# Tail of an encoder layer: where the last rows are scaled, added and summed

## The chip, the cores and the metric

The kernel runs on one core of one Trainium2 chip. A core has a matrix engine (TensorE, "PE" in the profile), three engines for elementwise work (VectorE or "DVE", ScalarE or "ACT", GpSimd or "POOL"), a queue engine that only issues transfers (SyncE, "SP"), an on-chip memory of 128 partitions (SBUF) and accumulation banks behind TensorE (PSUM). The metric is device time in microseconds of the whole program.

## The reference

The reference is one layer of an encoder on 512 positions of width 1024, in float32:

```python
h = _rmsnorm(x, g_pre_mix)
...                                  # retention and gating branches, merged
x = x + _rmsnorm(merged @ w_out, g_post_mix)
h2 = _rmsnorm(x, g_pre_ffn)
x = x + _rmsnorm(_conv_gated_mlp(h2, w_up, conv_w, conv_b, w_down), g_post_ffn)
```

with `_rmsnorm(y, g) = y / sqrt(mean(y*y) + EPS) * g` along each row. Only the last line concerns us. Call the result of `w_down` y, and x after the first half x1. Each row of the output is `x1 + y * g_post_ffn * (mean(y*y) + EPS) ** -0.5`.

## The kernel before

The 512 positions are four token tiles of 128 rows, t = 0 to 3; a row's 1024 columns are two halves of 512. Weights stream from DRAM through SyncE's queue; ScalarE and VectorE split every float32 matrix into a high and a low part, and TensorE multiplies three products of those parts for each tile. Some of the products use a Strassen-like scheme with seven products, whose results are then combined by VectorE.

The output matrix of the MLP is made in two column halves. The first half (columns 0 to 511) is finished early: `first_share` (L1418) multiplies it by `g_post_ffn` into a tile `zg[t]` and puts its mean of squares into column 0 of the small tile `qn[t]`. The second half (columns 512 to 1023) is finished at the very end, tile by tile, by `token(t)` (L1434), in the order 0, 2, 1, 3. Each call

- loads the two halves of x1 of this tile from DRAM (`xt`, L1440, on SyncE's queue);
- lets TensorE add the last 24 products to two banks, 12 for each quarter of 256 columns (`add_whole`, L1370);
- `sums(i)` for quarter i: VectorE adds bank and earlier part into z (L1452), and ScalarE squares z and sums along the row into column 2 + i of `qn[t]` (L1454). An ACTIVATE with a sum shows in the trace as two instructions, the second an accumulator read;
- `weighted(i)`: VectorE multiplies z by `g_post_ffn` into `zs_` (L1459);
- `first_sum`: VectorE adds column 2 and EPS to column 0 (L1462, one element per row);
- `scale`: VectorE adds column 3 (`s_2`, L1469), and POOL raises it to the power -0.5 (`sc`, named `qr` in the trace, L1470);
- `rows(t', ...)` for the tile t' before it: VectorE computes `zg * sc + x1` and `zs_ * sc + x1` in place, one instruction per half (L1502; the last tile's second half in two quarters), and stores each piece on SyncE's or ScalarE's queue (L1505).

After the last tile `rows` is called for it too. So the rows of tile 0 are made during tile 2, those of tile 2 during tile 1, those of tile 1 during tile 3.

A scheduler orders the instructions of each engine when the program is built, by trace order and by when it thinks that operands are ready. `tc.keep_in_program_order` (called `pin` here) queues an instruction behind the one that was traced before it on its engine; it is applied in tiles 1 and 3 to VectorE's instructions. `tc.issue_after(ins)` queues all instructions of a block, on `ins`'s engine, behind `ins`, without waiting for it to finish. Every engine runs its instructions in the order given; waits between engines are semaphores. Tiles of SBUF named by `blk` come from a pool of 66 buffers that are taken again when their last reader is done.

Of the kernel before, what the change touches and what calls it, by code (L numbers as in the profile page):

```python
# [12 lines left out]
AF = mybir.ActivationFunctionType  # L13
ALU = mybir.AluOpType

P = 128
D = 1024
S = 512
NT = S // P
# [30 lines left out]
def tile_block(ctx: ExitStack, tc, xT, x, wall, par, cs, wsp, bsp, gpost, gffn, out):  # L50
    nc = tc.nc
# [6 lines left out]
    def nm(s):  # L58
        uid[0] += 1
        return f"{s}_{uid[0]}"  # L60

    def blk(dt=F32, n="blk", shape=(P, S)):
        return sb.tile(list(shape), dt, tag="blk", bufs=NBLK, name=nm(n))
# [17 lines left out]
    def tmp(n="tmp", shape=(P, S)):  # L81
        return sb.tile(list(shape), F32, tag="tmp", bufs=6, name=nm(n))

    def halves(n):
        return [blk(n=n), blk(n=n)]

    def small(n, w, bufs=2):
        return sb.tile([P, w], F32, tag=n, bufs=bufs, name=nm(n))
# [4 lines left out]
    def const(n, shape):  # L93
        return sb.tile(list(shape), F32, tag=n, bufs=1, name=n)
# [4 lines left out]
    def two(t):  # L99
        return t.rearrange("p (n c) -> p n c", n=2)  # L100
# [5 lines left out]
    def in_turn(o):  # L106
        return o.rearrange("p (c n) -> p n c", n=2)
# [16 lines left out]
    i = 0  # L124
    while i < NW:
        pair = [(f, i) for f in FORMS]
        if i == SV0:
# [3 lines left out]
            i = U0  # L131
# [6 lines left out]
        elif i == UP0 + 2 * COUPLES[0][0]:  # L138
# [3 lines left out]
            i = UP0 + 2 * COUPLES[-1][1] + 2  # L142
# [10 lines left out]
    v = nc.vector  # L153
# [123 lines left out]
    def w_get(look=LOOK):  # L277

        i = w_pos[0]
        w_pos[0] += 1  # L280
        room = 2 * look + (2 if w_size(units[i]) == 2 else 0)
        n = sum(w_size(u) for u in units[i : w_pos[1]])
        while w_pos[1] < len(units) and (w_pos[1] <= i or n + w_size(units[w_pos[1]]) <= max(room, 9 if look == LOOK else 0)):
            u = units[w_pos[1]]
            w_ready[w_pos[1]] = w_unit(u)
            w_pos[1] += 1
            n += w_size(u)
        return w_ready.pop(i)
# [106 lines left out]
    for k in range(KD):  # L395
# [4 lines left out]
        xt = xts[k]  # L400
# [55 lines left out]
    for t in range(NT):  # L456
        for n in range(2):
            xt = blk(n="x0")
            nc.sync.dma_start(xt, x[t, :, n * S : (n + 1) * S])
            nc.scalar.activation(  # L460
                out=xt, in_=xt, func=AF.Square, accum_out=ss[:, 4 * n + t : 4 * n + t + 1]
# [18 lines left out]
    for c in range(19, 1, -2):  # L480
        v.scalar_tensor_tensor(
            out=lc, in0=lc, scalar=1.0 / c, in1=lb, op0=ALU.add, op1=ALU.mult
        )
    v.scalar_tensor_tensor(out=lc, in0=lc, scalar=1.0, in1=la, op0=ALU.add, op1=ALU.mult)
    with behind():
        v.tensor_scalar(out=lg, in0=lgt, scalar1=0.0, scalar2=None, op0=ALU.min)
    v.scalar_tensor_tensor(
        out=lg, in0=lc, scalar=-2.0, in1=lg, op0=ALU.mult, op1=ALU.add
# [12 lines left out]
    for i, op in enumerate((ALU.max, ALU.min)):  # L501
        v.tensor_scalar(
            out=near[:, i * P : (i + 1) * P], in0=dist[:, P : 2 * P], scalar1=0.0, scalar2=None, op0=op
# [5 lines left out]
    zt = const("zt", [P, H, NT])  # L509
# [465 lines left out]
    for j in range(UW):  # L975
# [3 lines left out]
        i = v.tensor_mul(two(u), in_turn(o), two(rbc)).ins  # L979
# [135 lines left out]
    x1 = [[dp_.tile([P, S], F32, tag=f"x1_{t}{n}", name=f"x1_{t}{n}") for n in range(2)] for t in range(NT)]  # L1115
# [36 lines left out]
    def turn(t, zs):  # L1152
        c = slice(t * 64, (t + 1) * 64)
        pf = []
        for n in range(2):
            p = ps()
            for f in range(4):
                pf.append(p[:, f * P : (f + 1) * P])
                nc.tensor.transpose(pf[-1], zs[n][:, f * P : (f + 1) * P], ident)
        for k in range(KD):  # L1160
            high = nc.scalar.activation(
                out=two(h2h[k])[:, :, c], in_=in_turn(pf[k]), func=AF.Copy, scale=col(FFNG + k)
            )
        for k in range(KD):
            last = v.scalar_tensor_tensor(
                out=two(h2l[k])[:, :, c], in0=in_turn(pf[k]), scalar=col(FFNG + k), in1=as32(two(h2h[k])[:, :, c]),
                op0=ALU.mult, op1=ALU.subtract,
            )
        return pf, high.ins, last.ins
# [26 lines left out]
    for t in range(NT):  # L1196
        acc = [dn_.finish(t, 0)]
        if t > 1:
            rows, _, last = turn(t - 2, zs[t - 2])
            if t == 2:  # L1200
                h2_rows(0, rows)
            with tc.issue_after(last):
                zs[t - 1] = scaled(*zs[t - 1])
        acc.append(dn_.finish(t, 1))
        zs[t], squared, ended = norms(t, acc)
        if t == 0:
            zs[0] = scaled(*zs[0])
    with tc.issue_after(squared):
        h2_rows(1, rows)
# [103 lines left out]
    i = 0  # L1313
# [46 lines left out]
    def add_whole(m, t, gs, ws, last=False):  # L1360

        c = slice(t * P, (t + 1) * P)
        for n, b in enumerate(((M2, M3), (M4, M8))[t // 2]):
            o = m[b][:, (t % 2) * 256 : (t % 2 + 1) * 256]
            for g, (wh, wl) in zip(gs, ws):
                for k in range(2):
                    f = slice(k * S + n * 256, k * S + (n + 1) * 256)
                    ah, al = whole[2 * g + k]
                    for i, (a_, w_) in enumerate(((ah, wh), (ah, wl), (al, wh))):
                        nc.tensor.matmul(  # L1370
                            o, a_[:, c], turns(w_[:, f]), start=b == M8 and t == 2 and g == k == i == 0,
                            stop=last and g == gs[-1] and k == 1 and i == 2, skip_group_check=True,
                        )
# [41 lines left out]
    qn = [small("q", 4, 4) for _ in range(NT)]  # L1415
# [13 lines left out]

    m, ww = {}, []  # L1430
    e1, uu, xx, yy = (blk(n="e") for _ in range(4))
    ahead = []

    def token(t):  # L1434

        if not ww:
            ww.extend([w_get(), w_get()])
        xt = halves("x1")
        for n in range(2):
            nc.sync.dma_start(xt[n], x1[t][n])  # L1440
        add_whole(m, t, (0, 1), ww, True)
        z, zs_ = blk(n="z"), blk(n="zs")
        last, ahead[:] = list(ahead), []
        banks = (((M2, e1), (M3, xx)), ((M4, uu), (M8, yy)))[t // 2]
        halves_ = slice(0, 256), slice(256, 512)
        end = t in (1, NT - 1)
        pin = tc.keep_in_program_order if end else (lambda i: i)

        def sums(i):
            b, e = banks[i]  # L1450
            f = halves_[t % 2]
            pin(v.tensor_add(z[:, halves_[i]], m[b][:, f], e[:, f]))  # L1452
            j = tmp("junk")
            nc.scalar.activation(  # L1454
                out=j[:, :256], in_=z[:, halves_[i]], func=AF.Square, scale=D ** -0.5, accum_out=qn[t][:, 2 + i : 3 + i]
            )

        def weighted(i):
            pin(v.tensor_mul(zs_[:, halves_[i]], z[:, halves_[i]], gpf[1][:, halves_[i]]))  # L1459

        def first_sum():
            pin(v.scalar_tensor_tensor(  # L1462
                out=qn[t][:, 0:1], in0=qn[t][:, 2:3], scalar=EPS, in1=qn[t][:, 0:1], op0=ALU.add, op1=ALU.add
            ))

        sc, s_2 = small("qr", 1, 4), small("qs", 1, 4)

        def scale():
            pin(v.tensor_add(s_2, qn[t][:, 0:1], qn[t][:, 3:4]))  # L1469
            nc.gpsimd.tensor_tensor(out=sc, in0=s_2, in1=nhalf[:, 0:1], op=ALU.pow)  # L1470

        sums(0)
        if t == NT - 1:
            weighted(0)
            sums(1)
            first_sum()
            rows(*last, (0,), pin)
            scale()
            rows(*last, (1,), pin)
            weighted(1)  # L1480
        else:
            weighted(0)
            first_sum()
            if end:
                rows(*last, (0,), pin)
            sums(1)
            if last:
                rows(*last, (1,) if end else (0,), pin)
            scale()
            weighted(1)  # L1490
            if last and not end:
                rows(*last, (1,))
        ahead[:] = t, xt, zs_, sc

    def rows(t, xt, zs_, sc, which, pin=lambda i: i):

        zt = (zg[t], zs_)
        for i, (a, b) in enumerate(((0, 512), (512, 768), (768, 1024)) if t == NT - 1 else ((0, 512), (512, 1024))):
            if a // S in which:
                f = slice(a % S, a % S + b - a)  # L1500
                o = zt[a // S][:, f]
                pin(v.scalar_tensor_tensor(  # L1502
                    out=o, in0=o, scalar=sc, in1=xt[a // S][:, f], op0=ALU.mult, op1=ALU.add
                ))
                (nc.sync, nc.scalar)[i % 2].dma_start(out[t, :, a:b], o)  # L1505

    def after6():
        v.tensor_add(uu, m[M6], e1)
        v.tensor_sub(xx, m[M5], uu)
        token(0)  # L1510
# [15 lines left out]
    for t in (2, 1, 3):  # L1526
        token(t)
# [133 lines left out]
```

## Time and profile before

| | us |
|---|---|
| median of 3 runs | 785.31 (785.30 to 785.34) |
| the profiled execution | 785.08 |
| its span | 783.3 |
| TensorE busy | 775.6 |
| VectorE busy | 626.5 |
| ScalarE busy | 467.8 |
| POOL busy | 104.0 |

The span is the time from the first to the last recorded instruction; the execution is 1.78 us longer than it. Times in the views are microseconds from the span's start. A timeline row gives start, duration, engine, line of the code, operation, and written from read tiles with their shapes; brackets hold the idle time ahead of it and what ended it. A row with "x2" merges two instructions. "SPq" and "ACTq" are queues on which transfers are issued, so such a row shows the issue and not the transfer itself.

### The profile page before, as it was taken

Reading aid. Unit: us, or ns where it says so; the run is one execution under the profiler, and the core shown is the slowest. Engines: PE = TensorE matmul, PEld = TensorE weight load, DVE = VectorE, ACT = ScalarE, POOL = GpSimd, SP = SyncE. Lnnn points to the kernel's source line nnn. Section 1 sums busy time; section 2 is a strip of 40 time slices with the busy share of each in tenths; the row PEclk is TensorE's granted clock in tenths of the full one; section 3 lists DMA queues with packets and bytes.
Section 4 is the critical chain, followed back from the end, with each engine's and each line's share of the span. In section 5 each row is a group of like instructions: output and inputs, shape, how many; then the busy total and the mean of one; then the engine's idle time right before and its main releaser. Section 6 shows DMA issues by size and latency. Waiting matters only on the chain.

```text
span 783.3 us, 13258 instructions
## 1 busy us (share of the span) xinstructions
PE 775.6 (99%) x5067; PEld 720.3 (92%) x5067; DVE 626.5 (80%) x1067; ACT 467.8 (60%) x848; POOL 104.0 (13%) x132
## 2 busy tenths in 40 slices
PE   9999999999999999999999999999999999999996
PEld 8888998998899999999998998999999998999996
DVE  7467887788786877867765679989999889877987
ACT  7555558689385544444444776657777578644542
POOL 0040001130012111032211200001111012200001
PEclk9999999999999999999999999999999999999999
DMA  8782224453123333223459111425555365632244
GB/s 293 260 266 88 81 82 162 108 133 126 55 106 108 108 108 108 106 84 108 138 161 344 57 69 39 122 108 141 141 149 149 108 196 114 170 114 108 108 162 162
DMA packets 35889, 104.78 MB, mean 134 GB/s; under 512 B 4401, under 2 KB 6321, under 8 KB 35825
## 3 DMA queue, kind: packets, MB, share of 16 engines
q1 hardware_dynamic: 27936, 87.81, 31.8%
q0 software_dynamic: 7024, 14.95, 9.0%
q10 hardware_dynamic: 864, 1.18, 0.4%
q8 instruction: 39, 0.64, 0.3%
q14 instruction: 26, 0.20, 0.1%
HBM read 91.34 MB, written 4.19 MB: 122 GB/s over the span
## 4 chain that ended last, share of the span: by engine, by line
PE 98%; DVE 1%; ACT 0%; POOLq 0%; issue 0%; POOL 0%; DVEq 0%
PE ps L917 22%; PE ps L291 13%; PE ps L293 13%; PE ps L292 13%; PE ps L1354 11%; PE ps L746 5%; PE ps L625 4%; PE ps L627 4%; PE ps L626 4%; PE ps L1089 2%; PE ps L1091 2%; PE ps L1090 2%; PE ps L1370 2%; PE ps L1011 1%; PE ps L411 1%; PE ps L393 0%
## 5 line engine op out<-in xcount | busy, mean ns | idle before, releaser
L116 DVE TENSOR_TENSOR wl<-raw,wh 128x1024 fp32r<-128x1024 f32 (+1 forms) x88 | 100.6, 1152 | 56.1 <-issue 20.6
L97 ACT ACTIVATE wf<-raw 128x512 fp32r<-128x512 f32 x126 | 75.6, 624 | 83.8 <-PE ps L292 37.1
L97 ACT ACTIVATE wh<-raw 128x1024 fp32r<-128x1024 f32 (+2 forms) x92 | 89.1, 981 | 28.9 <-DMA raw<-wall 15.5
L917 PE MATMUL ps<-sh,wf 128*128 128x256 f32 x576 | 105.3, 275 | 0.0
L116 DVE TENSOR_TENSOR wf<-raw,wf 128x512 fp32r<-128x512 f32 x126 | 93.3, 754 | 14.9 <-ACT wf L97 14.7
L917 PEld LDWEIGHTS ps<-sh,wf 128*128 128x128 f32 x576 | 91.7, 192 | 0.8 <-ACT u L97 0.2
L291 PE MATMUL ps<-h2h,wh 128*128 128x512 f32 (+1 forms) x256 | 90.7, 354 | 0.0
L293 PE MATMUL ps<-h2h,wl 128*128 128x512 f32 (+1 forms) x256 | 90.4, 353 | 0.0
L292 PE MATMUL ps<-h2l,wh 128*128 128x512 f32 (+1 forms) x256 | 90.4, 353 | 0.0
L917 PE MATMUL ps<-sl,wf 128*128 128x256 f32 x288 | 79.3, 275 | 0.0
L1354 PE MATMUL ps<-dh,fh 128*128 128x256 f32 x216 | 59.5, 276 | 0.0
L1354 PE MATMUL ps<-dh,fl 128*128 128x256 f32 x216 | 59.5, 275 | 0.0
L1354 PE MATMUL ps<-dl,fh 128*128 128x256 f32 x216 | 59.4, 275 | 0.0
L917 PEld LDWEIGHTS ps<-sl,wf 128*128 128x128 f32 x288 | 55.3, 192 | 0.4
L97 ACT ACTIVATE dh<-raw 128x768 fp32r<-128x768 f32 (+1 forms) x36 | 33.6, 950 | 33.5 <-DVE raw L224 17.6
L293 PEld LDWEIGHTS ps<-h2h,wl 128*128 128x128 f32 x256 | 48.6, 190 | 5.1
L291 PEld LDWEIGHTS ps<-h2h,wh 128*128 128x128 f32 x256 | 48.7, 190 | 4.5
L292 PEld LDWEIGHTS ps<-h2l,wh 128*128 128x128 f32 x256 | 48.7, 190 | 4.4
L627 PE MATMUL ps<-wh,xl 128*128 128x512 f32 x128 | 48.6, 379 | 0.0
L626 PE MATMUL ps<-wl,xh 128*128 128x512 f32 x128 | 48.5, 379 | 0.0
L625 PE MATMUL ps<-wh,xh 128*128 128x512 f32 x128 | 48.5, 380 | 0.0
L917 PE MATMUL ps<-xh,wf 128*128 128x256 f32 x240 | 43.8, 276 | 0.0
(343 smaller groups left out, 2185.8 us busy)
## 6 DMA issues: line engine op xcount, KB each, us to landing
raw<-wall SPq DMA_DIRECT2D x144, 512.0 KB, 3.6
x<-x SPq DMA_DIRECT2D x24, 256.0 KB, 5.9
fl<-gp POOLq DMA_DIRECT2D x12, 256.0 KB, 4.0
swap<-qkraw POOLq DMA_DIRECT2D x16, 128.0 KB, 4.3
x<-x POOLq DMA_DIRECT2D x8, 256.0 KB, 2.3
fl<-fs POOLq DMA_DIRECT2D x8, 256.0 KB, 3.3
xT<-xT SPq DMA_DIRECT2D x7, 256.0 KB, 5.5
xT<-xT POOLq DMA_DIRECT2D x4, 256.0 KB, 4.0
```

The lines of the kernel that those rows point to most:

```text
L97: return nc.scalar.activation(out=o, in_=i, func=AF.Copy)
L116: low[0] = nc.vector.tensor_sub(lo, src, as32(hi)).ins
L291: nc.tensor.matmul(o, ah, bh, start=start, stop=False, skip_group_check=skip)
L292: nc.tensor.matmul(o, ah, bl, start=False, stop=False, skip_group_check=skip)
L293: nc.tensor.matmul(o, al, bh, start=False, stop=stop, skip_group_check=skip)
L625: nc.tensor.matmul(acc[t], xh[k][:, c], turns(wh[:, f]), start=k == 0, stop=False)
L626: nc.tensor.matmul(acc[t], xh[k][:, c], turns(wl[:, f]), start=False, stop=False)
L627: part_end[0] = nc.tensor.matmul(acc[t], xl[k][:, c], turns(wh[:, f]), start=False, stop=k == KD - 1)
L746: nc.tensor.matmul(bank[t], a_[:, c], turns(w_[:, f]), start=first and k == i == 0, stop=last and k == 3 and i == 2, skip_group_check=True,)
L917: self.last = nc.tensor.matmul(o, w_[:, c], a_, start=first and k == n == 0, stop=k == 3 and n == 2, skip_group_check=True,)
L1089: nc.tensor.matmul(o, ah, turns(bh), start=k == 0, stop=False)
L1354: nc.tensor.matmul(o, a_[:, c], turns(w_[:, f]), start=j == t == i == 0, stop=j == DP - 1 and i == 2 and n not in (M2, M3, M4), skip_group ...
```

## The change

Three things are changed, all in the tail:

1. Tile 0's rows are no longer made by VectorE. ScalarE scales each half in place (`Copy` with `sc` as scale), and a transfer issued by POOL adds x1 into it, straight from DRAM (`accum_op=ALU.add`). x1 of tile 0 is therefore not loaded into SBUF. The two finished halves are stored by SyncE, in tile 3, queued behind the loads of x1 for tile 3.
2. In tile 3, the rows of tile 1 are placed otherwise among the pinned instructions: the first half ahead of `sums(0)`, the second half ahead of `sums(1)`. Before, both came behind `sums(1)`.
3. In tile 3, the squares of the last quarter are summed on VectorE: `tensor_tensor_reduce` multiplies z by itself, scales by 1/1024, adds up along the row starting from column 0 of `qn[t]`, and writes `s_2`. ScalarE's square and VectorE's addition of column 3 go; `first_sum` now comes between `z` and this instruction.

```diff
     e1, uu, xx, yy = (blk(n="e") for _ in range(4))
-    ahead = []
+    ahead, kept = [], []
 
     def token(t):
 
         if not ww:
             ww.extend([w_get(), w_get()])
-        xt = halves("x1")
-        for n in range(2):
-            nc.sync.dma_start(xt[n], x1[t][n])
+        xt = halves("x1") if t else x1[t]
+        for n in range(2 if t else 0):
+            loaded = nc.sync.dma_start(xt[n], x1[t][n]).ins
+        if t == NT - 1:
+            with tc.issue_after(loaded):
+                for n in range(2):
+                    nc.sync.dma_start(out[0, :, n * S : (n + 1) * S], kept[0][n])
         add_whole(m, t, (0, 1), ww, True)
...
+        sc, s_2 = small("qr", 1, 4), small("qs", 1, 4)
+
         def sums(i):
             b, e = banks[i]
             f = halves_[t % 2]
             pin(v.tensor_add(z[:, halves_[i]], m[b][:, f], e[:, f]))
             j = tmp("junk")
+            if t == NT - 1 and i:
+                first_sum()
+                pin(v.tensor_tensor_reduce(
+                    out=j[:, :256], in0=z[:, halves_[i]], in1=z[:, halves_[i]], scale=1.0 / D, scalar=qn[t][:, 0:1],
+                    op0=ALU.mult, op1=ALU.add, accum_out=s_2,
+                ))
+                return
...
-        sc, s_2 = small("qr", 1, 4), small("qs", 1, 4)
-
         def scale():
-            pin(v.tensor_add(s_2, qn[t][:, 0:1], qn[t][:, 3:4]))
+            if t < NT - 1:
+                pin(v.tensor_add(s_2, qn[t][:, 0:1], qn[t][:, 3:4]))
             nc.gpsimd.tensor_tensor(out=sc, in0=s_2, in1=nhalf[:, 0:1], op=ALU.pow)
 
-        sums(0)
         if t == NT - 1:
+            rows(*last, (0,), pin)
+            sums(0)
             weighted(0)
+            rows(*last, (1,), pin)
             sums(1)
-            first_sum()
-            rows(*last, (0,), pin)
             scale()
-            rows(*last, (1,), pin)
             weighted(1)
         else:
+            sums(0)
             weighted(0)
             first_sum()
             if end:
...
     def rows(t, xt, zs_, sc, which, pin=lambda i: i):
 
         zt = (zg[t], zs_)
+        if t == 0:
+            for n in which:
+                nc.scalar.activation(out=zt[n], in_=zt[n], func=AF.Copy, scale=sc)
+                nc.gpsimd.dma_start(zt[n], xt[n], accum_op=ALU.add)
+            kept.append(zt)
+            return
```

## The prediction

> **What bounds the kernel now.** I read three views: the page, for what carries the span as a whole; the chain of waits of the last 20 us, because the change touches only the tail; then the timelines of VectorE, TensorE, POOL, ScalarE and SP there.
>
> ```profile
> PE 775.6 (99%) x5067; PEld 720.3 (92%) x5067; DVE 626.5 (80%) x1067; ACT 467.8 (60%) x848; POOL 104.0 (13%) x132
> PE 98%; DVE 1%; ACT 0%; POOLq 0%; issue 0%; POOL 0%; DVEq 0%
> ```
>
> TensorE carries the program, and the change removes nothing from it. In the tail it is otherwise. "z(t,n)" is L1452 for token tile t and half n, "w(t,n)" the weighting L1459, "rows(t,n)" L1502, "q" L1462, "s_2" L1469. The tiles go 0, 2, 1, 3. TensorE:
>
> ```profile
> 769.42 0.28 PE L1370 MATMUL ps<-wh,fl 128*128 128x256 f32 x1
> 770.76 0.28 PE L1370 MATMUL ps<-wh,fl 128*128 128x256 f32 x1
> 772.10 0.28 PE L1370 MATMUL ps<-wh,fl 128*128 128x256 f32 x1
> 776.12 0.28 PE L1370 MATMUL ps<-wh,fl 128*128 128x256 f32 x1
> ```
>
> These are the last matmuls for z(2,0), z(2,1), z(1,0) and z(3,1); the last one ends at 776.40. VectorE, from tile 0's rows on:
>
> ```profile
> 768.58 0.69 DVE L1514 TENSOR_TENSOR e<-ps,e 128x512 f32<-128x512 f32 x1
> 769.35 0.75 DVE L1502 SCALAR_TENSOR_TENSOR zg<-zg,qr,x 128x512 f32<-128x512 f32 x1
> ...
> 770.35 0.75 DVE L1502 SCALAR_TENSOR_TENSOR zs<-zs,qr,x 128x512 f32<-128x512 f32 x1
> ...
> 772.41 0.16 DVE L1469 TENSOR_TENSOR qs<-q 128x1 f32<-128x1 f32 x1
> 772.49 0.42 DVE L1452 TENSOR_TENSOR z<-ps,e 128x256 f32<-128x256 f32 x1
> 772.94 0.42 DVE L1459 TENSOR_TENSOR zs<-z,gpf 128x256 f32<-128x256 f32 x1
> 773.48 0.16 DVE L1462 SCALAR_TENSOR_TENSOR q<-q 128x1 f32<-128x1 f32 x1
> 773.57 0.75 DVE L1502 SCALAR_TENSOR_TENSOR zg<-zg,qr,x 128x512 f32<-128x512 f32 x1
> 774.24 0.42 DVE L1452 TENSOR_TENSOR z<-ps,e 128x256 f32<-128x256 f32 x1
> 774.58 0.74 DVE L1502 SCALAR_TENSOR_TENSOR zs<-zs,qr,x 128x512 f32<-128x512 f32 x1
> 775.24 0.16 DVE L1469 TENSOR_TENSOR qs<-q 128x1 f32<-128x1 f32 x1
> 775.31 0.42 DVE L1459 TENSOR_TENSOR zs<-z,gpf 128x256 f32<-128x256 f32 x1
> 775.64 0.42 DVE L1452 TENSOR_TENSOR z<-ps,e 128x256 f32<-128x256 f32 x1
> 776.10 0.43 DVE L1459 TENSOR_TENSOR zs<-z,gpf 128x256 f32<-128x256 f32 x1
> 776.44 0.42 DVE L1452 TENSOR_TENSOR z<-ps,e 128x256 f32<-128x256 f32 x1
> 776.78 0.15 DVE L1462 SCALAR_TENSOR_TENSOR q<-q 128x1 f32<-128x1 f32 x1
> 776.84 0.74 DVE L1502 SCALAR_TENSOR_TENSOR zg<-zg,qr,x 128x512 f32<-128x512 f32 x1
> 777.51 0.16 DVE L1469 TENSOR_TENSOR qs<-q 128x1 f32<-128x1 f32 x1
> 777.58 0.74 DVE L1502 SCALAR_TENSOR_TENSOR zs<-zs,qr,x 128x512 f32<-128x512 f32 x1
> 778.25 0.42 DVE L1459 TENSOR_TENSOR zs<-z,gpf 128x256 f32<-128x256 f32 x1
> 778.77 0.75 DVE L1502 SCALAR_TENSOR_TENSOR zg<-zg,qr,x 128x512 f32<-128x512 f32 x1
> ```
>
> The reader is to see that VectorE hardly pauses from 773.48 to 778.67 (778.25 + 0.42). z(3,1) starts at 776.44, 0.04 behind the last matmul, and at the same moment VectorE comes free (0.34 behind w(3,0)): both limits meet there. Behind it, rows(1,0) at 776.84 and rows(1,1) at 777.58 fill the time in which ScalarE squares z(3,1) and POOL takes the root: they cost nothing where they stand. The rest of the tail:
>
> ```profile
> 775.54 0.60 POOL L1470 TENSOR_TENSOR qr<-qs,nhalf 128x1 f32<-128x1 f32 x1 [2.27 <-DVE qs L1469]
> 777.81 0.93 POOL L1470 TENSOR_TENSOR qr<-qs,nhalf 128x1 f32<-128x1 f32 x1 [1.67 <-DVE qs L1469]
> 776.95 0.42 ACT L1454 ACTIVATE junk<-z 128x256 f32<-128x256 f32 x1 [0.28 <-DVE q L1462]
> 777.27 0.20 ACT L1454 ACTIVATION_READ_ACCUMULATOR junk<-z 128x1 f32 x1
> 780.34 0.33 SPq L1505 DMA_DIRECT2D out<-zs  x1
> ```
>
> The chain is z(3,1), square, s_2, root, rows(3) from 778.77, store at 780.34; from z(3,1) to rows(3,0) it takes 2.33 us.
>
> **The change, part by part.**
>
> *Tile 0's rows leave VectorE.* Two instructions go (0.75 each, 769.35 and 770.35), 1.5 us of VectorE work. How much reaches the end? z(2,1) can then start right behind its matmuls (770.76 + 0.28 = 771.04, before at 771.42). z(1,0) cannot start before 772.10 + 0.28 = 772.38; with the 0.04 lag that is 772.42, against 772.49 before. So 0.07 of the 1.5 us is left; the remainder turns into waiting for TensorE. Bounds: 0 (a longer lag) to 0.07; I take 0.05, close to the lag seen at z(3,1).
>
> *The same rows on ScalarE and POOL.* The nearest rows:
>
> ```profile
> L97 ACT ACTIVATE wf<-raw 128x512 fp32r<-128x512 f32 x126 | 75.6, 624 | 83.8 <-PE ps L292 37.1
> L264 POOL DMA_DIRECT2D sb<-wall x4 | 3.6, 1072 | 12.0 <-DVE sl L116 10.7 <-ACT sh L97 1.3
> sb<-wall POOLq DMA_DIRECT2D x4, 256.0 KB, 6.0
> 772.72 0.55 POOL L1470 TENSOR_TENSOR qr<-qs,nhalf 128x1 f32<-128x1 f32 x1 [3.40 <-DVE qs L1469]
> 770.47 0.42 ACT L1454 ACTIVATE junk<-z 128x256 f32<-128x256 f32 x1 [2.45 <-DVE z L1452]
> 770.69 1.85 SPq L1440 DMA_DIRECT2D x<-x  x4
> ```
>
> Two copies of 0.62 from 769.35 (tile 0's scale is there, as its row on VectorE shows) end near 770.6. ScalarE had idled 2.45 us before 770.47, so the square of tile 2 slips by about 0.1; its sum is wanted at 772.4. L264 is the same kind of transfer, 256 KB from DRAM added into SBUF: 1.07 us of POOL each, 6.0 to landing. POOL would issue from about 770.0 to 772.1, and the next root is wanted at 772.4: cost 0, covered by POOL's idle time. Without this cover (rival C) it is dear. The sums land by about 777; both stores wait on SP for them, and behind those the stores of tiles 2, 1 and 3. The last of these is issued near 780 or later, so cost 0. Two loads of 256 KB fall away; tile 1's and 3's loads are issued from 770.69 at the latest known, or earlier since there is less ahead of them: cost 0.
>
> *The new order in tile 3.* All its VectorE instructions are pinned in program order. Now rows(1,0) stands ahead of z(3,0), and rows(1,1) ahead of z(3,1). But rows(1,0) needs tile 1's root, which ended at 775.54 + 0.60 = 776.14. With 0.05 gained: root 776.09, rows(1,0) 776.12. VectorE idles from about 775.6, where z(3,0) stood before. Then by the spacings above: z(3,0) + 0.67 = 776.79 (776.84 to 777.51); w(3,0) + 0.46 = 777.25; rows(1,1) + 0.34 = 777.59; z(3,1) + 0.67 = 778.26. That is 1.82 later than before, and TensorE has been done for 1.9 us. The two rows instructions are no longer hidden: they stand in front of the chain that they used to fill.
>
> *One instruction sums the squares.* Gone are square, accumulator read and s_2 (776.95 to 777.67); q now comes behind z(3,1): 778.60, and the sum waits for its result: 778.60 + 0.16 + 0.03 = 778.79. The trace has no such sum. Bounds: 0.42 (a 128x256 product, L1459) and 0.75 (twice as many elements, L1502); I take 0.52, since ScalarE's square and accumulator read take 0.52 together (776.95 to 777.47) against 0.42 for the square alone. It ends at 779.31. The root starts 0.14 behind s_2 in the rows (777.67 to 777.81): 779.45. Its price lies between 0.55 and 0.93; the 0.93 had rows(1,1), 0.74 long, running beside its start, the 0.55 and 0.60 only w or z. Beside it now is only w(3,1), so 0.58: 780.03, rows(3,0) at 780.06. From z(3,1) the chain takes 1.80 instead of 2.33: 0.53 won.
>
> [...]
>
> **Sum.** 1.82 - 0.53 = +1.29 (780.06 - 778.77), and behind rows(3,0) nothing changes. A second count of VectorE: 0.45 idle at rows(1,0), 0.4 idle under the last root (0.1 before), some 0.2 of dependent gaps and 0.45 of new sum against s_2, less 0.05 at the start: about +1.3 too. Span 783.3 + 1.3 = 784.6; the profiled execution took 785.08, so 786.37. The median, 785.31, lies 0.23 above that execution: 786.6, or +0.16%. A measurement of this kernel can tell about 0.2%, 1.57 us, from no change: my forecast is a small loss inside it.
>
> **The rivals.**
>
> *B, the sum or the last root dearer.* The sum costs 0.75, or the root 0.93: +1.5 to +1.9, 786.8 to 787.2. For it: neither has an exact row. Against: VectorE's L1502 reads two SBUF operands 512 wide in 0.75, only 0.06 more than L1514, as wide with one operand in PSUM (0.69); and long work of VectorE no longer stands beside the root. The sum costs 0.23 more at 0.75 (chance 0.10), the root 0.35 more at 0.93 (0.08). [...]
>
> *C, slower by more: the root of tile 2 gets stuck.* If ScalarE's copies come behind tile 2's squares (771.08 + 0.45 + 0.52 = 772.05), the first transfer is issued from 772.67, ahead of that root on POOL, and rows(2,0) waits: 772.67 + 1.07 + 0.56 = 774.3 instead of 773.5. It decides once the root starts after 772.9; price about +0.75 on top, 787.3. Against: the copies are ready at 769.35, tile 2's first z not before 769.42 + 0.28 + 0.04 + 0.42 = 770.16.
>
> *D, the new order costs nothing.* Were tile 1's root early enough for both rows to fit ahead of 776.40, only the shorter chain stays: -0.5, 784.8. Against: they need 2 x 0.67 and the root ended at 776.14.
>
> *E, the 1.5 us reach the end.* 785.31 - 1.5 = 783.8. Against: 772.38.
>
> **Chances.** Forecast 0.55 (0.07 of it above 786.88), B 0.18 (0.12 above), C 0.15 (0.14 above), D 0.07, E 0.05 (0.02 of it faster by over 0.2%). So faster 0.02, within 0.65, slower 0.33. The forecast's own range is 786.3 to 786.9 (sum 0.42 to 0.65, root 0.55 to 0.65); with B and most of C 785.7 to 787.4, which leaves out D, E and the top of C.
>
> **What would show it.** Right: VectorE idle before rows(1,0) near 776.1; z(3,1) near 778.3, with nothing of TensorE within 1.5 us; z(3,1) to rows(3,0) about 1.8. Wrong: z(3,1) near 776.5 (D), rows(2,0) after 774 (C), a sum of 0.7 or a last root of 0.9 (B). What would upset it all is another order on VectorE than the pins give.

## The result, and the profile after

The changed kernel takes 786.39 us (median of 22 runs, 785.76 to 787.24), the kernel before 785.33 (median of 22 runs beside them, 784.47 to 786.13). The ratio is 1.0015, with a 95% interval of 1.0008 to 1.0021: slower by 0.6 to 1.6 us, and within 0.2% by its median. The forecast was 786.6.

The ratios in this document leave out two single executions that took 1365.76 us (old order put back, below) and 2903.89 us (sum alone).

The profiled execution took 786.03, with a span of 784.2. Executions of one kernel differ by more than the change does to the tail (the 22 runs of before lie 1.66 us apart, the tail changes by 1.25), and in the nine profiles of this document the last matmul ends anywhere between 775.95 and 779.30; here it came 0.45 us earlier than in the profile of before. So I compare the tail from the end of the last matmul on, and call X the time from there to the start of rows(3,0). Line numbers move with each edit: in after, z is L1458, w L1472, q L1475, the sum L1462, rows L1520, the root L1482, tile 0's copies L1512 and its adding transfers L1513. First the busy times and the chain of the page of after, then rows of the timeline of its TensorE and VectorE (start, duration, instruction):

```profile
PE 774.9 (99%) x5067; PEld 719.2 (92%) x5067; DVE 626.0 (80%) x1066; ACT 468.3 (60%) x848; POOL 105.5 (13%) x134
...
PE 98%; DVE 1%; DMA 0%; ACT 0%; issue 0%; POOLq 0%; POOL 0%; ACTq 0%; DVEq 0%
```

```profile
775.67 0.28 PE L1370 MATMUL ps<-wh,fl 128*128 128x256 f32 x1
771.96 0.42 DVE L1458 TENSOR_TENSOR z<-ps,e 128x256 f32<-128x256 f32 x1
...
774.79 0.42 DVE L1472 TENSOR_TENSOR zs<-z,gpf 128x256 f32<-128x256 f32 x1
775.65 0.75 DVE L1520 SCALAR_TENSOR_TENSOR zg<-zg,qr,x 128x512 f32<-128x512 f32 x1 [0.44 <-POOL qr L1482]
776.32 0.42 DVE L1458 TENSOR_TENSOR z<-ps,e 128x256 f32<-128x256 f32 x1
776.77 0.42 DVE L1472 TENSOR_TENSOR zs<-z,gpf 128x256 f32<-128x256 f32 x1
777.12 0.74 DVE L1520 SCALAR_TENSOR_TENSOR zs<-zs,qr,x 128x512 f32<-128x512 f32 x1
777.78 0.41 DVE L1458 TENSOR_TENSOR z<-ps,e 128x256 f32<-128x256 f32 x1
778.11 0.15 DVE L1475 SCALAR_TENSOR_TENSOR q<-q 128x1 f32<-128x1 f32 x1
778.30 0.48 DVE L1462 CUSTOM_DVE_ANT_0 junk<-z,q 128x256 f32<-128x256 f32 x1
778.71 0.08 DVE L1462 DVE_READ_ACCUMULATOR2_ANT qs<- 128x1 f32 x1
778.71 0.42 DVE L1472 TENSOR_TENSOR zs<-z,gpf 128x256 f32<-128x256 f32 x1
779.57 0.75 DVE L1520 SCALAR_TENSOR_TENSOR zg<-zg,qr,x 128x512 f32<-128x512 f32 x1 [0.44 <-POOL qr L1482]
```

The last matmul ends at 775.67 + 0.28 = 775.95. VectorE then is in the middle of rows(1,0), which it began 0.44 us late because it waited for tile 1's root. z(3,1) starts at 777.78, which is 1.83 behind the last matmul (0.04 before). From there to rows(3,0) it takes 1.79 (2.33 before). X is 779.57 - 775.95 = 3.62, against 2.37: a loss of 1.25 in the tail. Behind rows(3,0) hardly anything changes: to the end of the span 4.63, before 4.53, with spans given to 0.1.

The other engines in the timeline of after, and two rows of its transfers (KB of each, us from issue to landing):

```profile
768.90 0.72 ACT L1512 ACTIVATE zg<-zg,qr 128x512 f32<-128x512 f32 x1 [1.33 <-POOL qr L1482]
769.53 0.71 ACT L1512 ACTIVATE zs<-zs,qr 128x512 f32<-128x512 f32 x1
769.98 0.91 POOL L1513 DMA_DIRECT2D zg<-x  x1 [1.12 <-ACT zg L1512]
770.60 1.21 POOL L1513 DMA_DIRECT2D zs<-x  x1
772.05 0.56 POOL L1482 TENSOR_TENSOR qr<-qs,nhalf 128x1 f32<-128x1 f32 x1 [0.24 <-DVE qs L1481]
775.02 0.60 POOL L1482 TENSOR_TENSOR qr<-qs,nhalf 128x1 f32<-128x1 f32 x1 [2.41 <-DVE qs L1481]
778.93 0.60 POOL L1482 TENSOR_TENSOR qr<-qs,nhalf 128x1 f32<-128x1 f32 x1 [3.32 <-DVE qs L1462]
775.88 0.33 SPq L1444 DMA_DIRECT2D out<-zs  x1
```

```profile
zg<-x POOLq DMA_DIRECT2D x1, 256.0 KB, 3.9
zs<-x POOLq DMA_DIRECT2D x1, 256.0 KB, 5.3
```

Tile 0's copies and adding transfers run where they were expected, and POOL is free 0.24 us before the next root is wanted. Tile 0's second half is stored at 775.88, long before the last store.

### The profile page after: what moved, and what is told of

Same layout as the page of the kernel before. It is cut to its first block, busy times and chain, and to the rows that moved or that the text cites. A ratio compares the mean times of both kernels' runs of the same rounds, so it can differ in the third digit from the quotient of the medians.

```text
span 784.2 us, 13253 instructions
## 1 busy us (share of the span) xinstructions
PE 774.9 (99%) x5067; PEld 719.2 (92%) x5067; DVE 626.0 (80%) x1066; ACT 468.3 (60%) x848; POOL 105.5 (13%) x134
## 4 chain that ended last, share of the span: by engine, by line
PE 98%; DVE 1%; DMA 0%; ACT 0%; issue 0%; POOLq 0%; POOL 0%; ACTq 0%; DVEq 0%
PE ps L917 22%; PE ps L291 13%; PE ps L292 13%; PE ps L293 13%; PE ps L1354 11%; PE ps L746 5%; PE ps L625 4%; PE ps L627 4%; PE ps L626 4%; PE ps L1370 2%; PE ps L1090 2%; PE ps L1089 2%; PE ps L1091 2%; PE ps L1011 1%; PE ps L411 1%; PE ps L818 0%
```

## The experiments

All seven kernels compute the whole layer. This table takes X from each timeline; the ratio is to the kernel before, run beside it.

| kernel | z(3,1) behind the last matmul | z(3,1) to rows(3,0) | X | ratio, 95% interval |
|---|---|---|---|---|
| before | 0.04 | 2.33 | 2.37 | |
| after | 1.83 | 1.79 | 3.62 | 1.0015 (1.0008 to 1.0021) |
| old order put back in after | 0.03 | 2.60 | 2.63 | 1.0002 (0.9993 to 1.0011) |
| order alone | 1.90 | 2.32 | 4.22 | 1.0023 (1.0014 to 1.0032) |
| tile 0 alone | 0.03 | 2.34 | 2.37 | 1.0001 (0.9992 to 1.0010) |
| sum alone | 0.04 | 2.59 | 2.63 | 1.0005 (0.9996 to 1.0014) |
| z and w of tile 3 first, in after | 1.29 | 1.79 | 3.08 | 1.0015 (1.0006 to 1.0024) |
| w(3,1) first, in before | 0.04 | 2.14 | 2.18 | 1.0002 (0.9993 to 1.0011) |
| order alone, store elsewhere | 1.90 | 2.00 | 3.90 | 1.0017 (1.0005 to 1.0030) |

A ratio's interval here is some 0.7 us to either side, so the ratios tell the order's kernels from before and not one small step from another. X tells those apart, from one profiled execution each; the reading relies on X. Kernels with the same order and the same instructions behind the last matmul repeat it to the hundredth (2.37 twice, 2.63 twice).

### The old order put back in the changed kernel

```diff
         if t == NT - 1:
-            rows(*last, (0,), pin)
             sums(0)
             weighted(0)
-            rows(*last, (1,), pin)
             sums(1)
+            rows(*last, (0,), pin)
             scale()
+            rows(*last, (1,), pin)
             weighted(1)
```

> The changed kernel with tile 1's rows put back behind z(3,1); tile 0's rows on ScalarE and the sum on VectorE stay. Let X be the time from the end of the last matmul to the start of rows(3,0): 2.37 us before (776.40 to 778.77), 3.62 after (775.95 to 779.57). Theory 1 (the new order costs): z(3,1) starts 0.04 behind the last matmul again; behind it VectorE has q, the sum, rows(1,0), rows(1,1) and w(3,1) to do: 0.33 + 0.19 + 0.41 + 0.67 + 0.67 + 0.34 = 2.61, so X about 2.65, 0.3 more than before and 1.0 less than after; time about 785.6. Theory 2 (the transfers that add, or the sum, are what costs; the order does nothing): X stays at 3.6 and the time at 786.4.

Rows of its timeline:

```profile
776.22 0.28 PE L1370 MATMUL ps<-wh,fl 128*128 128x256 f32 x1
776.53 0.42 DVE L1458 TENSOR_TENSOR z<-ps,e 128x256 f32<-128x256 f32 x1
...
777.47 0.75 DVE L1520 SCALAR_TENSOR_TENSOR zg<-zg,qr,x 128x512 f32<-128x512 f32 x1
778.13 0.75 DVE L1520 SCALAR_TENSOR_TENSOR zs<-zs,qr,x 128x512 f32<-128x512 f32 x1
778.79 0.42 DVE L1472 TENSOR_TENSOR zs<-z,gpf 128x256 f32<-128x256 f32 x1
779.13 0.74 DVE L1520 SCALAR_TENSOR_TENSOR zg<-zg,qr,x 128x512 f32<-128x512 f32 x1
...
777.69 0.93 POOL L1482 TENSOR_TENSOR qr<-qs,nhalf 128x1 f32<-128x1 f32 x1 [1.52 <-DVE qs L1462]
```

z(3,1) starts 0.03 behind the last matmul (776.50) again, and X is 779.13 - 776.50 = 2.63. The order is worth 0.99 of X in the changed kernel, as theory 1 has it. The root ends at 778.62 and nobody waits for it: VectorE hardly pauses from z(3,1) to rows(3,0), which starts 0.34 behind w(3,1).

### The order alone, in the kernel before

```diff
-        sums(0)
         if t == NT - 1:
+            rows(*last, (0,), pin)
+            sums(0)
             weighted(0)
+            rows(*last, (1,), pin)
             sums(1)
             first_sum()
-            rows(*last, (0,), pin)
             scale()
-            rows(*last, (1,), pin)
             weighted(1)
         else:
+            sums(0)
             weighted(0)
```

> The kernel before with only the new order of tile 1's rows in tile 3. Theory 1: rows(1,0) waits for tile 1's root (776.14 before) and z(3,1) comes 2.13 behind rows(1,0), about 1.90 behind the last matmul; then ScalarE's square, s_2 and the root, 1.91: X about 3.8, so 1.4 more than before; time about 786.8, slower than the whole change, since the shorter chain of the new sum is missing. Theory 2: X stays at 2.4, time 785.3.

Rows of its timeline:

```profile
779.02 0.28 PE L1370 MATMUL ps<-wh,fl 128*128 128x256 f32 x1
781.20 0.42 DVE L1452 TENSOR_TENSOR z<-ps,e 128x256 f32<-128x256 f32 x1
781.53 0.15 DVE L1462 SCALAR_TENSOR_TENSOR q<-q 128x1 f32<-128x1 f32 x1
...
783.52 0.75 DVE L1503 SCALAR_TENSOR_TENSOR zg<-zg,qr,x 128x512 f32<-128x512 f32 x1 [0.44 <-POOL qr L1470]
...
781.31 0.34 ACTq L1506 DMA_DIRECT2D out<-zs  x1
782.05 0.42 ACT L1454 ACTIVATE junk<-z 128x256 f32<-128x256 f32 x1 [1.28 <-DVE q L1462]
```

z(3,1) comes 781.20 - 779.30 = 1.90 late, as expected, and the order alone is the slowest of all. (This profiled execution took 789.84, where the median is 787.29; its last matmul ended 2.90 later than in before, so the excess lies ahead of the tail and X is free of it.) But X is 4.22 and not 3.8: the square starts at 782.05, while z(3,1) was done at 781.62 and q at 781.68. Ahead of it on ScalarE stands the issue of the store of rows(1,1), 781.31 to 781.65. A later experiment takes that store away.

### Tile 0's rows alone, in the kernel before

```diff
-        xt = halves("x1")
-        for n in range(2):
-            nc.sync.dma_start(xt[n], x1[t][n])
+        xt = halves("x1") if t else x1[t]
+        for n in range(2 if t else 0):
+            loaded = nc.sync.dma_start(xt[n], x1[t][n]).ins
...
+        if t == 0:
+            for n in which:
+                nc.scalar.activation(out=zt[n], in_=zt[n], func=AF.Copy, scale=sc)
+                nc.gpsimd.dma_start(zt[n], xt[n], accum_op=ALU.add)
...
```

with the two stores behind the loads, as in the change.

> The kernel before with only tile 0's rows moved to ScalarE and transfers that add. Theory 1: z(1,0) waits for its matmuls instead of VectorE, z(3,1) starts 0.04 behind the last matmul as before, so X is 2.30 to 2.37 and the time 785.3: the 1.5 us of VectorE that are saved are worth nothing. Rival E of the prediction: 1.4 us less, 783.9. Theory 2 (the transfers cost): X above 2.6 and the time above 785.6.

```profile
776.11 0.28 PE L1370 MATMUL ps<-wh,fl 128*128 128x256 f32 x1
769.72 0.42 DVE L1456 TENSOR_TENSOR z<-ps,e 128x256 f32<-128x256 f32 x1 [0.47 <-PE ps L1370]
771.10 0.16 DVE L1466 SCALAR_TENSOR_TENSOR q<-q 128x1 f32<-128x1 f32 x1 [0.50 <-ACT junk L1458]
...
776.42 0.42 DVE L1456 TENSOR_TENSOR z<-ps,e 128x256 f32<-128x256 f32 x1
...
778.76 0.75 DVE L1512 SCALAR_TENSOR_TENSOR zg<-zg,qr,x 128x512 f32<-128x512 f32 x1
```

X is 778.76 - 776.39 = 2.37, the value of before to the hundredth. The 1.5 us that VectorE saves turn up as waiting: 0.47 for TensorE at z(2,0), then 0.50 at q of tile 2 for ScalarE's square, which stands behind the two copies there. Rival E (783.9) and the theory that the transfers cost are both out.

### The sum alone, in the kernel before

```diff
+            if t == NT - 1 and i:
+                first_sum()
+                pin(v.tensor_tensor_reduce(
+                    out=j[:, :256], in0=z[:, halves_[i]], in1=z[:, halves_[i]], scale=1.0 / D, scalar=qn[t][:, 0:1],
+                    op0=ALU.mult, op1=ALU.add, accum_out=s_2,
+                ))
+                return
...
```

with the old order of tile 3 kept, and with the sum in place of ScalarE's square and of s_2, as in the change.

> The kernel before with only the last quarter's squares summed in one VectorE instruction, old order. Theory 1 (VectorE is what the tail waits for): the sum adds about 0.4 us of VectorE's work behind z(3,1), so X is about 2.65, 0.3 more than before, time 785.6; moved from ScalarE, the square stands in the way of the rows it used to run beside. Rival: the chain of z, sum and root sets the end, and it is shorter by 0.5: X about 1.85, time 784.8.

```profile
776.72 0.28 PE L1370 MATMUL ps<-wh,fl 128*128 128x256 f32 x1
777.04 0.42 DVE L1454 TENSOR_TENSOR z<-ps,e 128x256 f32<-128x256 f32 x1
...
779.63 0.74 DVE L1509 SCALAR_TENSOR_TENSOR zg<-zg,qr,x 128x512 f32<-128x512 f32 x1
```

X is 779.63 - 777.00 = 2.63: 0.26 worse. In the old order VectorE's own work sets the end behind z(3,1), and the square is then better left on ScalarE. A shorter chain (the rival, 1.85) is no use where the chain does not bind.

### z and w of tile 3 first, in the changed kernel

```diff
-            rows(*last, (0,), pin)
             sums(0)
             weighted(0)
+            rows(*last, (0,), pin)
             rows(*last, (1,), pin)
             sums(1)
```

> The changed kernel with z(3,0) and w(3,0) put ahead of rows(1,0), so that VectorE need not idle for tile 1's root; both rows stay ahead of z(3,1). In the changed kernel VectorE idled 0.44 there, and z(3,1) came 1.83 behind the last matmul. Theory 1 (the order costs by what stands ahead of z(3,1), the idle time being a part): z(3,0) at about 775.13, w(3,0) 775.58, rows(1,0) 775.92, rows(1,1) 776.59, z(3,1) 777.26 in the changed kernel's times, 1.31 behind the last matmul; X (last matmul to rows(3,0)) falls from 3.62 to about 3.10, still 0.7 over the kernel before; time about 786.0. Rival (the wait for the root is the whole loss): X near 2.4, time 785.3.

```profile
776.30 0.28 PE L1370 MATMUL ps<-wh,fl 128*128 128x256 f32 x1
776.55 0.74 DVE L1520 SCALAR_TENSOR_TENSOR zg<-zg,qr,x 128x512 f32<-128x512 f32 x1
777.87 0.41 DVE L1458 TENSOR_TENSOR z<-ps,e 128x256 f32<-128x256 f32 x1
...
779.66 0.75 DVE L1520 SCALAR_TENSOR_TENSOR zg<-zg,qr,x 128x512 f32<-128x512 f32 x1 [0.44 <-POOL qr L1482]
```

The idle time ahead of rows(1,0) is gone, and X falls by 0.54 to 779.66 - 776.58 = 3.08. The rest of the delay stays: two rows instructions, 1.32 from the start of the first to z(3,1), stand ahead of a bank that has been ready since 776.58. So the wait for the root is not the whole loss.

### w(3,1) ahead of rows(1,1), in the kernel before

```diff
             scale()
-            rows(*last, (1,), pin)
             weighted(1)
+            rows(*last, (1,), pin)
```

> The kernel before with w(3,1) ahead of rows(1,1): the same instructions, another pair of them beside the last root. Theory 1 (a root on POOL waits for the VectorE instruction with two SBUF operands that runs when it starts, and gets in before the next one): it waits for w(3,1), which ends 0.4 earlier than rows(1,1) does, and takes 0.56 to 0.65 instead of 0.93; rows(3,0) is then bound by VectorE's own work, X 2.20 instead of 2.37. Rival (a root gets in only when VectorE's run of such instructions pauses): it waits for rows(1,1) behind w(3,1), takes about 1.3, X 2.7.

```profile
776.17 0.28 PE L1370 MATMUL ps<-wh,fl 128*128 128x256 f32 x1
777.63 0.42 DVE L1459 TENSOR_TENSOR zs<-z,gpf 128x256 f32<-128x256 f32 x1
777.97 0.74 DVE L1502 SCALAR_TENSOR_TENSOR zs<-zs,qr,x 128x512 f32<-128x512 f32 x1
778.63 0.74 DVE L1502 SCALAR_TENSOR_TENSOR zg<-zg,qr,x 128x512 f32<-128x512 f32 x1
...
777.86 0.60 POOL L1470 TENSOR_TENSOR qr<-qs,nhalf 128x1 f32<-128x1 f32 x1 [1.67 <-DVE qs L1469]
```

The root takes 0.60 instead of 0.93 and X is 778.63 - 776.45 = 2.18, 0.19 below the kernel before and the shortest tail of all. In time that does not show (1.0002, with 0.07% to the lower side). The root ends at 778.46, 0.41 behind the end of w(3,1) (778.05), though rows(1,1) had started by then.

### The order alone, with tile 1's second store on SyncE's queue

```diff
-                (nc.sync, nc.scalar)[i % 2].dma_start(out[t, :, a:b], o)
+                (nc.sync, nc.scalar)[i % 2 if t != 1 else 0].dma_start(out[t, :, a:b], o)
```

> The kernel with the order alone, and the store of tile 1's second half moved from ScalarE's queue to SyncE's. With the order alone X was 4.22 instead of the expected 3.8, and the square of z(3,1) began at 782.05, 0.4 behind both z(3,1) and the store issued ahead of it on ScalarE at 781.31. Theory 1 (the store's issue ahead of the square holds ScalarE for 0.35 and some 0.4 more): without it the square begins 0.03 to 0.1 behind z(3,1), X 3.8, time 786.9. Rival (the square waits for something else): X stays 4.2.

```profile
776.37 0.28 PE L1370 MATMUL ps<-wh,fl 128*128 128x256 f32 x1
778.55 0.41 DVE L1452 TENSOR_TENSOR z<-ps,e 128x256 f32<-128x256 f32 x1
778.88 0.15 DVE L1462 SCALAR_TENSOR_TENSOR q<-q 128x1 f32<-128x1 f32 x1
780.55 0.75 DVE L1503 SCALAR_TENSOR_TENSOR zg<-zg,qr,x 128x512 f32<-128x512 f32 x1 [0.44 <-POOL qr L1470]
...
779.06 0.42 ACT L1454 ACTIVATE junk<-z 128x256 f32<-128x256 f32 x1 [0.94 <-DVE q L1462]
```

The square now starts 0.51 behind z(3,1)'s start, where it started 0.85 behind it with the store ahead. X falls from 4.22 to 780.55 - 776.65 = 3.90. The store was the cause of 0.32 of the miss. Of the remaining 0.1 over my 3.8, 0.06 is that 0.51: in tiles 2 and 1 a square starts 0.45 behind its z (774.94 behind 774.49). The profile names q as what ended the wait, and the square does start 0.03 behind the end of q (779.03). But tile 3's first square has no q ahead of it and comes 0.51 behind its z as well (777.60 behind 777.09). So what makes the squares of tile 3 later stays open.

This kernel has the new order and no sum on VectorE, and from z(3,1) to rows(3,0) it takes 2.00, against 2.33 before. So 0.33 of the 0.54 that the whole change wins on this stretch comes with the order, which takes the long rows instruction away from the last root (0.60 here beside w(3,1), 0.93 before beside rows(1,1)); the sum itself is worth the other 0.21 (2.00 to 1.79; tile 0 alone leaves the stretch as it was, 2.34).

## Why the prediction was right

**Tile 0's rows.** Right in what it is worth: I took 0.05 of the 1.5 us, at most 0.07. Measured from the last matmul, z(1,0) moved from 3.91 ahead of it to 3.99: 0.08. Tile 0 alone left X where it was. Less right in where the rest goes: I had it all turn into waiting for TensorE, but 0.50 of it is waiting for ScalarE. Tile 2's square came 0.12 later than before, measured from the last matmul (770.14 in after, 770.47 before), as I had forecast with 0.1. VectorE was now ahead of it, though, and q, which needs that square, stood in front of z(2,1). So z(2,1) started at 770.74, 0.15 behind its matmuls, and not right behind them. It cost nothing, because z(1,0) had to wait for its own matmuls anyway: they ended at 771.93, and it started at 771.96.

The covers held, in part by luck. The two copies took 0.72 and 0.71, but the next instruction started 0.63 and 0.61 behind each, which is the 0.62 of the forecast. In before's times POOL began to issue at 770.43 and not 770.0, and the two issues took 1.83 us and not 2.14. These two errors work against each other, so POOL was free 0.24 us ahead of the next root, where the forecast had 0.3.

**The order in tile 3.** Right, and the cause of the loss. Rows(1,0) waited for the root with 0.44 of idle time, and z(3,1) was 1.79 later, where the sum had 1.82. Undoing the order alone gives back 0.99. One remark ahead of that sum was too strong: that rows(1,0) and rows(1,1) cost nothing behind z(3,1). The last root took 0.93 there beside rows(1,1) and 0.60 beside w(3,1), and putting w(3,1) first won 0.19 of X. They cost little there, not nothing.

**The sum.** Right in size: 778.30 to 778.79 is 0.49, forecast 0.52 between 0.42 and 0.75; the last root took 0.60, forecast 0.58; together 1.79 from z(3,1) to rows(3,0), forecast 1.80. But the text booked the whole 0.53 that this stretch wins under the sum. The order alone with the store elsewhere shows that 0.33 of the measured 0.54 comes without the sum, by the shorter root, and 0.21 with it. Nor did the text say that the gain exists only under the new order. Under the old one the same instruction costs 0.26.

**The total.** The tail grew by 1.25, forecast 1.29; the medians by 1.06, forecast 1.3. One by one from the kernel before, tile 0 gives 0.00, the sum +0.26 and the order +1.85, which add up to more than the whole. From the order alone to the whole change X falls by 0.60: 0.07 ahead of z(3,1) (1.90 to 1.83) and 0.53 behind it (2.32 to 1.79), of which 0.32 is the square that no longer queues behind a store on ScalarE: 1.85 - 0.07 - 0.53 = 1.25. I put the 0.07 down to tile 0, since nothing else differs ahead of z(3,1); no kernel had the order and tile 0 without the sum.

**The rivals.** B did not come: neither the sum nor the root was dear. The sum's 256 elements took 0.48, against 0.42 for a plain product of that size, and the root took 0.60. C did not come: the copies ran ahead of tile 2's squares (768.90 and 769.53, the first square 770.14), and the root started on time (772.05, 0.15 behind the end of its s_2). D is excluded by the new order itself (the root was 0.33 ahead of the last matmul, and both rows need 1.32). E is excluded by tile 0 alone.

**The last root beside VectorE.** The root ended 0.40 to 0.42 behind the end of the VectorE instruction with two SBUF operands that ran when it started: 778.74 behind rows(1,1) in before, 779.53 behind w(3,1) in after, 778.46 behind w(3,1) with the weights first. With one operand in PSUM it was otherwise. In before tile 0's root started while L1514 (`e<-ps,e`) ran, 768.58 to 769.27; it took 0.56 and ended 0.05 behind it:

```profile
768.76 0.56 POOL L1470 TENSOR_TENSOR qr<-qs,nhalf 128x1 f32<-128x1 f32 x1 [84.89 <-DVE qs L1469]
```

And a root that had started did not hold VectorE up: in before a root runs from 772.72 to 773.27, and w(1,0) starts within it, at 772.94, 0.03 behind z(1,0), and takes its usual 0.42.

## What to carry to other kernels

Ask of each instruction that is moved what it was filling: rows(1,0) and rows(1,1) cost little behind z(3,1) (0.19 of X came back with w(3,1) ahead of rows(1,1)), where they fill most of the time in which VectorE would have waited for ScalarE and POOL, and 1.3 us ahead of it. Work taken from a busy engine is worth only what is left before its next wait for another engine; follow the engine forward to that wait before counting it (here 0.08 of 1.5 us was left). And a shorter chain and less work on an engine are two different gains: where the engine's own work sets the end, moving another engine's work onto it loses (here 0.26).

## What was not expected

An issue of a store on ScalarE's queue held the next ACTIVATE for longer than the issue itself: the store was issued from 781.31 to 781.65, and the square, with z(3,1) and q done by 781.68, started at 782.05; with the store elsewhere the same square started 0.03 behind the end of q. This is one case, and what fills the 0.37 is not shown by these rows.

Whether a root would get in without a pause of VectorE was open. With the weights first, a root of one element per row on POOL took 0.60 beside two VectorE instructions that follow one another without a gap: rows(1,1) had started at 777.97, ahead of the end of w(3,1) at 778.05, and yet the root did not wait for it, but ended at 778.46, ahead of the end of rows(1,1) at 778.71. So of the instructions with two SBUF operands only the one that is running when the root starts matters, in the cases seen here.

The sum on VectorE shows as two instructions, 0.48 and 0.08; the next one of VectorE starts with the second, so in that engine's time it takes 0.41.
